# A longer lag for the mixer steps that run beside the products of a hybrid block

## The chip, the cores and the metric

The kernel runs on one core of one Trainium2 chip. The metric is the device time of one execution in microseconds. Of the kernel before, three runs are known, with a median of 3934.16 us.

## What is computed

Two blocks of two layers each work on one sequence of 1024 tokens with 1024 features. Block 1, which the change is about, runs three mixers side by side in each layer and joins them in one output product:

```python
def hybrid_layer(x, c_act, ...):
    h = rms_norm(x, pre_gain) * (1.0 + scale) + shift
    aq, ak, av, ag, rq, rk, rv, rg, gq, gk, gv, gg, ga = split(h @ w_in)
    a_out = sliding_window_attention(rotary(aq), rotary(ak), av, sinks) * silu(ag)
    r_out = rms_norm(retention(rotary(rq), rotary(rk), rv)) * silu(rg)
    g_out = rms_norm(gated_linear_attention(gq, gk, gv, log_a), gain) * silu(gg)
    y = concatenate([a_out, r_out, g_out]) @ w_out
    return x + gate * rms_norm(y, post_gain)
```

Attention looks back over a window of 128 tokens; retention and gated linear attention (GLA) carry a state from chunk to chunk. Block 2 (attention with a context, spatial gating, a Fourier mixer, and a squared ReLU network) follows on the result.

## The kernel before

Tokens are worked on in tiles of 128, four tiles to a group, so block 1 has four steps: two layers by two groups. All large products are made in float32 from two float32r parts, which gives three matmuls for each pair of operands. `product` (L467) walks over the eight 128-row slices of the inner dimension. For each slice it loads a weight tile into `wr`, makes its high part `wh` on ScalarE and its low part `wl` on VectorE (L202, L203), and issues the matmuls (L502), 12 for four outputs. After each slice it calls `tick`.

The mixers have no products of their own to wait in. They are generators in a list `bg`, and `tick` lets the first of them run up to its next `yield`. So a mixer's program is spread over the slices of the products that are made meanwhile: `s_attn` beside `p_ret`, `s_ret` beside `p_gla`, and `s_gla` beside the next step's `p_attn`, or, in the last step, beside two early products of block 2. A piece that feeds matmuls from VectorE or ScalarE runs one `yield` ahead of the piece that uses it: in `s_attn` `scores(i)` before `values(i - 1)`, in `s_ret` `values(i - 1)` before `into(i - 2)`, in `s_gla` `level(i)` before `scores(i - 1)`. `into` (L534) transposes a finished head and splits it into `mT`, the left operand of the output product. `aside` advances the modulation vectors (L311, L316, L317, L283), which are also worked on in the background.

The order of the instructions on each engine is not the program's order alone. A scheduler issues an instruction when it thinks its operands ready, and takes the earlier one in the program first where several are. Some pieces have a higher priority (`high_priority`): the weight splits most of all.

A tile's tag names its pool and the number of its buffers. The tags that matter here: `sc` for scores and other products of a mixer step, `st` for the GLA score matrices and masked queries, `pe` for temporaries of the evacuations (rotary, norm, gating), and in PSUM `mm` (4 banks) for the products, `sm` (2 banks) for scores, their transposes and state updates, `o` (1 bank) for the values. Stores of tiles to the device's memory are issued by POOL (L579), whose descriptors lie in a scratch that takes 16 KB of each partition unless a size is given.

A GLA unit `level` makes two differences on POOL (L983, L984), their exponential on ScalarE (L985), `kl` (L987) and `ql` (L989) on VectorE. `scores` multiplies them (L997) and copies the result under a mask into the score matrix (L1000). There are seven levels for each of two halves.

Of the kernel before, what the change touches and what calls it, by code (L numbers as in the profile page):

```python
# [25 lines left out]
GT = 4  # L26
# [136 lines left out]
class Net:  # L163
    HP, HE, HX = 3000, 800, 600

    def __init__(self, ctx, tc, a):
        self.tc, self.nc, self.a = tc, tc.nc, a
        self.ctx = ctx
        self.n = 0
        self.bg = []  # L170
        self.pools = {}
        mk = lambda name, tags, **kw: self.open(ctx, name, tags, **kw)
        self.cpool = ctx.enter_context(tc.tile_pool(name="cst", bufs=1))
        self.dpool = ctx.enter_context(tc.tile_pool(name="dr", bufs=1, space=DRAM))
        mk("small", {"ti": 14, "tm": 16, "md": 4, "ab": 6, "pad": 1})
        self.T("pad", [P, 8])
        mk("big", {"wr": 3, "wl": 4, "wh": 4, "x": 4, "pe": 3,
                   "H": 16, "M": 4, "pt": 8, "kv": 2})
        mk("ps", {"mm": 4, "mt": 1, "sm": 2, "o": 1}, space=PSUM)

# [526 lines left out]
    def s_attn(self, l, g, st, mT):  # L707
        nc = self.nc
# [63 lines left out]

        units = [(t, e) for t in range(GT) for e in range(2)]
        ready = []
        for i in range(len(units) + 1):
            if i < len(units):
                scores(*units[i])
                yield True
            if i:
                values(*units[i - 1])  # L780
                t, e = units[i - 1]
                if e:
                    ready.append((t, close(t)))
                elif ready:
                    self.into(mT, 0, ready[0][0], ready.pop(0)[1], 4)
                yield True
                if i % 4 == 3:
                    self.aside()
        yield True
        self.into(mT, 0, ready[0][0], ready[0][1], 4)  # L790

    def p_ret(self, l, g, hT, st):
        nc, w = self.nc, self.a["w_in"][l]
# [36 lines left out]
    def s_ret(self, l, g, st, mT):  # L830
        nc = self.nc
# [42 lines left out]
            return self.head_norm(O, sg[t])  # L874

        sc, y = [None] * GT, [None] * GT
        for i in range(GT + 2):
            if i > 1:
                self.into(mT, 4, i - 2, y[i - 2], 2)
            if 0 < i <= GT:  # L880
                y[i - 1] = values(i - 1, *sc[i - 1])
            if i < GT:
                sc[i] = scores(i)
            yield True
            if i in (2, 4):
                self.aside()
                yield True
# [47 lines left out]
    def s_gla(self, l, g, st, mT):  # L935
# [86 lines left out]
            return self.head_norm(O, sg[t])  # L1022

        units = [(u, n, s) for u in range(2) for n, s in enumerate((64, 32, 16, 8, 4, 2, 1))]
        y, made = [None] * GT, None
        for i in range(len(units) + 1):
            if i:
                scores(*units[i - 1], *made)
            if i < len(units):
                made = level(*units[i])  # L1030
            if i in (9, 11):
                y[i // 2 - 4] = values(i // 2 - 4)
            if i in (11, 13):
                self.into(mT, 6, i // 2 - 5, y[i // 2 - 5], 2)
            yield True
            if i % 7 in (2, 5):
                self.aside()
        for i in range(2, GT + 2):
            if i < GT:
                y[i] = values(i)  # L1040
            if i > 3:
                self.into(mT, 6, i - 2, y[i - 2], 2)
            yield True
            if i in (2, 4):
                self.aside()
# [5 lines left out]
    def block1(self, cur, n_layers, after=True):  # L1051
        a = self.a
        self.first = True
        with ExitStack() as ctx:
            self.open(ctx, "b1", {"gt": 2, "ys": 4, "ac": 1, "aw": 4, "pu": 12, "st": 3, "sc": 5, "rs": 2, "gs": 2, "gb": 2, "gq": 2, "dg": 2}, {"row": "x"})
            self.cpool = ctx.enter_context(self.tc.tile_pool(name="c1", bufs=1))
            self.cst1 = self.C(CST1.shape)
            self.load(self.cst1[:, :64], a["cst1"][:, :64])
# [671 lines left out]
```

## Time and profile before

| | us |
|---|---|
| median of three runs | 3934.16 |
| lowest and highest run | 3931.94, 3938.04 |
| the profiled execution | 3937.08 |
| its span, from the first to the last instruction | 3935.3 |
| TensorE busy | 3726.1 (95%) |
| VectorE busy | 2445.6 (62%) |
| ScalarE busy | 1685.8 (43%) |
| GpSimd (POOL) busy | 649.3 (17%) |

Busy times are sums over the whole span and say little about one stage. Block 1 takes about the first 1215 us of it. A wait is put down to the engine and instruction that ended it; matmuls follow each other in a pipeline, so a matmul's duration is longer than its distance to the next.

### The profile page before, as it was taken

To read this page: it belongs to the slowest core of one execution; us is meant where nothing else is said; L and a number is where in the kernel's file an instruction comes from. 1 tells how busy PE (TensorE), PEld (TensorE's weight loads), DVE (VectorE), ACT (ScalarE), POOL (GpSimd) and SP (SyncE) were. 2 spreads that over 40 slices of the span, in tenths; PEclk is the share of its full clock that TensorE was granted. 3 is DMA by queue.
4 is the path that set the end of the run, shared out by engine and by line. 5 is a ranking of instruction groups with operands and counts; after the bars stand their busy time and mean duration, and the time that the engine had idled before them with its cause. 6 is when DMAs were issued, how large, how long until landed. Compare 5 with 4: busy or idle time off the path is not lost. (4 is left out here: it accounts for less than half of the span.)

```text
span 3935.3 us, 55613 instructions
## 1 busy us (share of the span) xinstructions
PE 3726.1 (95%) x19144; PEld 3045.4 (77%) x19144; DVE 2445.6 (62%) x5209; ACT 1685.8 (43%) x3652; POOL 649.3 (17%) x1026
## 2 busy tenths in 40 slices
PE   7999999999999898899999999999899999999998
PEld 6877777877877787677887788888777788887886
DVE  7686787687687657576545643335765654455444
ACT  4443444454454555464334422224554543344333
POOL 2021134243252212131001000000311100001000
PEclk9999999999999999999999999999999999999999
DMA  6144344343343313333333632222412123334332
GB/s 213 50 134 121 113 143 121 109 129 110 105 136 98 103 56 107 108 108 105 126 102 110 209 110 68 62 66 89 145 54 86 69 64 97 97 100 166 97 97 94
DMA packets 249453, 420.37 MB, mean 107 GB/s; under 512 B 32002, under 2 KB 101203, under 8 KB 249171
## 3 DMA queue, kind: packets, MB, share of 16 engines
q1 hardware_dynamic: 241426, 389.52, 32.0%
q0 software_dynamic: 7744, 27.30, 1.9%
q8 instruction: 151, 2.47, 0.3%
q14 instruction: 132, 1.07, 0.1%
HBM read 389.42 MB, written 27.30 MB: 106 GB/s over the span
## 5 line engine op out<-in xcount | busy, mean ns | idle before, releaser
L203 DVE TENSOR_TENSOR wl<-wr,wh 128x512 fp32r<-128x512 f32 (+2 forms) x948 | 644.2, 682 | 812.9 <-ACT wh L202 809.4
L202 ACT CAST wh<-wr 128x512 fp32r<-128x512 f32 (+2 forms) x948 | 553.7, 585 | 1208.8 <-PE mm L502 489.8
L502 PE MATMUL mm<-wh,M 128*128 128x512 f32 (+1 forms) x2944 | 945.9, 393 | 24.6 <-ACT M L202 14.8
L502 PE MATMUL mm<-wh,H 128*128 128x512 f32 (+2 forms) x2432 | 791.5, 396 | 12.3 <-DVE pe L654 3.6
L506 PE MATMUL mm<-H,wh 128*128 128x512 f32 x2240 | 727.4, 395 | 1.8 <-ACT wh L202 1.7
L502 PEld LDWEIGHTS mm<-wh,M 128*128 128x128 f32 x2944 | 550.0, 190 | 142.8 <-ACT M L202 23.1
L502 PE MATMUL mm<-wl,M 128*128 128x512 f32 (+1 forms) x1472 | 576.0, 391 | 0.4 <-DVE wl L203 0.4
L502 PEld LDWEIGHTS mm<-wh,H 128*128 128x128 f32 x2432 | 450.0, 192 | 100.5 <-issue 4.7
L506 PEld LDWEIGHTS mm<-H,wh 128*128 128x128 f32 x2240 | 418.8, 189 | 82.2 <-ACT wh L202 2.0
L502 PE MATMUL mm<-wl,H 128*128 128x512 f32 (+2 forms) x1216 | 471.1, 388 | 0.0
L506 PE MATMUL mm<-H,wl 128*128 128x512 f32 x1120 | 444.5, 397 | 0.0
L502 PEld LDWEIGHTS mm<-wl,M 128*128 128x128 f32 x1472 | 279.8, 190 | 49.2 <-DVE wl L203 1.2
L502 PEld LDWEIGHTS mm<-wl,H 128*128 128x128 f32 x1216 | 234.0, 192 | 35.1 <-issue 0.2
L506 PEld LDWEIGHTS mm<-H,wl 128*128 128x128 f32 x1120 | 212.2, 189 | 37.2
L1398 PEld LDWEIGHTS o<-kv,pT 128*128 128x128 f32 x1280 | 158.1, 192 | 25.0 <-ACT pT L1394 20.4
L317 POOL TENSOR_TENSOR ac<-ac,aw 128x256 f32<-128x256 f32 x168 | 142.9, 851 | 162.8 <-ACT aw L316 143.9
L1398 PE MATMUL o<-kv,pT 128*128 128x64 f32 x1280 | 167.5, 274 | 1.6 <-ACT pT L1394 0.9
L311 DVE SCALAR_TENSOR_TENSOR ac<-aw,c,ac 128x256 f32<-128x256 f32 x280 | 160.1, 572 | 5.9 <-DMA aw<-in_w_ada 3.1
L1483 DVE TENSOR_TENSOR Z<-Z,mm 128x512 f32<-128x512 f32 x224 | 140.2, 681 | 2.8 <-PE mm L502 2.5
L558 POOL TENSOR_TENSOR tm<-tm 128x1 f32<-128x1 f32 x34 | 6.6, 196 | 763.3 <-ACT pe L553 762.9
L1375 DVE CUSTOM_DVE_ANT_0 p<-sm,c,c 128x384 f32<-128x384 f32 (+1 forms) x144 | 82.2, 571 | 76.0 <-PE sm L1373 74.5
L1381 ACT ACTIVATE p<-p,ti 128x640 f32<-128x640 f32 (+2 forms) x144 | 110.8, 770 | 43.1 <-DVE ti L1380 39.7
(353 smaller groups left out, 5703.1 us busy)
## 6 DMA issues: line engine op xcount, KB each, us to landing
wr<-in_w_ff SPq DMA_DIRECT2D x512, 256.0 KB, 2.7
wr<-in_w_in SPq DMA_DIRECT2D x240, 256.0 KB, 2.7
wr<-in_w_out SPq DMA_DIRECT2D x144, 256.0 KB, 2.7
x<-xd SPq DMA_DIRECT2D x64, 512.0 KB, 4.9
aw<-in_w_ada SPq DMA_DIRECT2D x192, 128.0 KB, 2.1
x<-in_w_ada SPq DMA_DIRECT2D x96, 256.0 KB, 2.9
xd<-x POOLq DMA_DIRECT2D x44, 512.0 KB, 3.8
wr<-in_w_in SPq DMA_DIRECT2D x152, 128.0 KB, 2.1
```

Of the source, the lines that this page charges most:

```text
L202: self.nc.scalar.copy(hi, src)
L203: self.nc.vector.tensor_sub(lo, src, hi.bitcast(F32))
L311: nc.vector.scalar_tensor_tensor(acc[:, 0], wt, c[0], acc[:, 0], ALU.mult, ALU.add)
L317: nc.gpsimd.tensor_tensor(acc[:, 1], acc[:, 1], wt, ALU.add)
L502: nc.tensor.matmul(acc[j][:, :ncol], lhsT=x[:, j * P:(j + 1) * P], rhs=y[:, :ncol], start=first, stop=last)
L506: nc.tensor.matmul(acc[j][:m, :w], lhsT=y[:, j * P:j * P + m], rhs=x[:, :w], start=first, stop=last)
L558: nc.gpsimd.tensor_tensor(ss[j][:, 0:1], ss[j][:, 0:1], ss[j][:, 1:2], ALU.add)
L1375: nc.vector.tensor_tensor_reduce(sc[:, at:at + w], ps[:, :w], mask, 1.0, prev, ALU.add, ALU.max, accum_out=acc)
L1381: nc.scalar.activation(sc[:, :at], sc[:, :at], AF.Exp, bias=nm, accum_out=den[:, h:h + 1])
L1398: nc.tensor.matmul(O[:, h * 64:h * 64 + 64], lhsT=pT[:, i, :], rhs=Vs(j)[:, sl], start=i == 0, stop=i == nk - 1)
L1483: nc.vector.tensor_add(y, y, ps)
```

## The change

Three mixers wait longer. In `s_attn` `values` runs two units behind `scores`, and `into` follows when the next tile closes. In `s_ret` `into` runs two steps behind `values`. In `s_gla` `scores` runs two levels behind `level`, kept in a list `made`, and `into` one step later. The calls of `aside` in `s_attn` leave the inner condition. The scratch for the descriptors shrinks from 16 KB to 4 KB per partition; the 12 KB go to one more `pe` buffer (2 KB), one more `st` (4 KB) and three more `sc` (2 KB each).

```diff
-        mk("big", {"wr": 3, "wl": 4, "wh": 4, "x": 4, "pe": 3,
+        mk("big", {"wr": 3, "wl": 4, "wh": 4, "x": 4, "pe": 4,
                    "H": 16, "M": 4, "pt": 8, "kv": 2})
...
-        for i in range(len(units) + 1):
+        for i in range(len(units) + 2):
             if i < len(units):
                 scores(*units[i])
                 yield True
-            if i:
-                values(*units[i - 1])
-                t, e = units[i - 1]
+            if i > 1:
+                values(*units[i - 2])
+                t, e = units[i - 2]
                 if e:
+                    if ready:
+                        self.into(mT, 0, *ready.pop(), 4)
                     ready.append((t, close(t)))
-                elif ready:
-                    self.into(mT, 0, ready[0][0], ready.pop(0)[1], 4)
                 yield True
-                if i % 4 == 3:
-                    self.aside()
+            if i % 4 == 3:
+                self.aside()
         yield True
-        self.into(mT, 0, ready[0][0], ready[0][1], 4)
+        self.into(mT, 0, *ready.pop(), 4)
...
-        for i in range(GT + 2):
-            if i > 1:
-                self.into(mT, 4, i - 2, y[i - 2], 2)
+        for i in range(GT + 3):
+            if i > 2:
+                self.into(mT, 4, i - 3, y[i - 3], 2)
...
-        y, made = [None] * GT, None
-        for i in range(len(units) + 1):
-            if i:
-                scores(*units[i - 1], *made)
+        y, made = [None] * GT, []
+        for i in range(len(units) + 2):
+            if i > 1:
+                scores(*units[i - 2], *made.pop(0))
             if i < len(units):
-                made = level(*units[i])
+                made.append(level(*units[i]))
             if i in (9, 11):
-                y[i // 2 - 4] = values(i // 2 - 4)
-            if i in (11, 13):
-                self.into(mT, 6, i // 2 - 5, y[i // 2 - 5], 2)
+                y[(i - 9) // 2] = values((i - 9) // 2)
+            if i in (12, 14):
+                self.into(mT, 6, (i - 12) // 2, y[(i - 12) // 2], 2)
...
-        for i in range(2, GT + 2):
+        for i in range(2, GT + 3):
             if i < GT:
                 y[i] = values(i)
-            if i > 3:
-                self.into(mT, 6, i - 2, y[i - 2], 2)
+            if i > 4:
+                self.into(mT, 6, i - 3, y[i - 3], 2)
...
-            self.open(ctx, "b1", {"gt": 2, "ys": 4, "ac": 1, "aw": 4, "pu": 12, "st": 3, "sc": 5, "rs": 2, "gs": 2, "gb": 2, "gq": 2, "dg": 2}, {"row": "x"})
+            self.open(ctx, "b1", {"gt": 2, "ys": 4, "ac": 1, "aw": 4, "pu": 12, "st": 4, "sc": 8, "rs": 2, "gs": 2, "gb": 2, "gq": 2, "dg": 2}, {"row": "x"})
...
-    nc = _bacc.Bacc("TRN2", target_bir_lowering=False, num_devices=1)
+    nc = _bacc.Bacc("TRN2", target_bir_lowering=False, num_devices=1, dynamic_dma_scratch_size=4096)
```

Every engine has the same instructions as before, in another order. Line numbers in the excerpts of the order are those of the kernel before; the changed functions keep them to within two lines, and the lines named here are the same in both.

First excerpt: VectorE in the second step, at the second GLA level. `sc_5684` is its `ql`, and the copy of its scores is the one that reads `sm_5705`. The L311 rows are modulation. Before:

```order
L989 TENSOR_TENSOR sc_5684<-st_5642,sc_5678 128x512
L311 SCALAR_TENSOR_TENSOR ac_5187<-aw_5191,c_70,ac_5187 128x256
L1000 COPY_PREDICATED st_5640<-c_629,sm_5674 128x8x64
L311 SCALAR_TENSOR_TENSOR ac_5187<-aw_5194,c_70,ac_5187 128x256
L1000 COPY_PREDICATED st_5640<-c_629,sm_5705 128x16x32
L311 SCALAR_TENSOR_TENSOR ac_5187<-aw_5197,c_70,ac_5187 128x256
L987 TENSOR_TENSOR sc_5713<-pt_4840,sc_5709 128x256
L311 SCALAR_TENSOR_TENSOR ac_5187<-aw_5200,c_70,ac_5187 128x256
L989 TENSOR_TENSOR sc_5715<-st_5642,sc_5709 128x512
```

With the change the same level's `ql` is `sc_5680`, and its scores are read from `sm_5779`:

```order
L989 TENSOR_TENSOR sc_5680<-st_5642,sc_5674 128x512
L1000 COPY_PREDICATED st_5640<-c_629,sm_5701 128x8x64
L311 SCALAR_TENSOR_TENSOR ac_5182<-aw_5189,c_70,ac_5182 128x256
L987 TENSOR_TENSOR sc_5709<-pt_4840,sc_5705 128x256
L311 SCALAR_TENSOR_TENSOR ac_5182<-aw_5192,c_70,ac_5182 128x256
L989 TENSOR_TENSOR sc_5711<-st_5642,sc_5705 128x512
L311 SCALAR_TENSOR_TENSOR ac_5182<-aw_5195,c_70,ac_5182 128x256
L1000 COPY_PREDICATED st_5640<-c_629,sm_5779 128x16x32
```

The next level's `ql` now stands ahead of the copy, where it stood behind it.

Second excerpt: TensorE in the third step's retention, from `values` of the second tile (L860, L862, into `o_4949`) to the transposes of the first tile's head `sc_4911` (L524). Before:

```order
L860 MATMUL o_4949<-rs_1934,sc_4930 128x128 x2
L862 MATMUL o_4949<-pu_4821,st_4921 128x64 x4
L502 MATMUL mm_5393<-wh_5396,H_2256 128x512
L502 MATMUL mm_5393<-wl_5397,H_2256 128x512
L502 MATMUL mm_5393<-wh_5396,H_2257 128x512
L524 MATMUL sm_4944<-c_76,sc_4911 128x128 x2
L867 MATMUL sm_4956<-pu_4821,pu_4411 128x128 x2
```

With the change, where the second tile's values go into `o_4944` (L506 is a product too, the last half of an output product):

```order
L862 MATMUL o_4944<-pu_4821,st_4921 128x64 x4
L846 MATMUL sm_4969<-pt_4414 128x128 x2
L506 MATMUL mm_4841<-H_2265,wh_5106 128x512
L506 MATMUL mm_4841<-H_2265,wl_5107 128x512
L506 MATMUL mm_4841<-H_2266,wh_5106 128x512
L506 MATMUL mm_4842<-H_2265,wh_5106 128x512
L506 MATMUL mm_4842<-H_2265,wl_5107 128x512
L846 MATMUL sm_4973<-pt_4414 128x128 x2
L506 MATMUL mm_4842<-H_2266,wh_5106 128x512
L502 MATMUL mm_5387<-wh_5391,H_2251 128x512
L283 MATMUL o_4991<-c_76,ac_4721 128x1 x2
L524 MATMUL sm_5032<-c_76,sc_4911 128x128 x2
```

The transposes stand behind the third tile's scores (L846), where they stood ahead of them.

## Rows read from the trace of the kernel before

**Rows 1.** The page: the span, and its part 1, the engines' busy time.
```profile
span 3935.3 us, 55613 instructions
...
PE 3726.1 (95%) x19144; PEld 3045.4 (77%) x19144; DVE 2445.6 (62%) x5209; ACT 1685.8 (43%) x3652; POOL 649.3 (17%) x1026
```

**Rows 2.** TensorE's waits, 100 to 1215 us: releaser; us in total, times, longest us.
```profile
PE sm L997 <- DVE sc L989: 19.6, 22, 2.4
PE sm L524 <- DVE sc L827: 10.8, 8, 1.9
PE o L1014 <- DVE st L1000: 6.0, 6, 2.2
PE mm L502 <- DVE pe L654: 3.6, 4, 2.5
PE sm L746 <- ACT sc L736: 3.0, 4, 1.1
...
PE mm L502 <- ACT wh L202: 0.8, 1, 0.8
```

**Rows 3.** Busy time by stretch: block 1, then four GLA stretches and their sum.
```profile
core 0: us, PE busy (x) PEld busy (x) DVE busy (x) ACT busy (x) POOL busy (x), PEclk, DMA share, GB/s
100.00:1215.00 1115.00, 1054.67 (x5677) 854.35 (x5675) 859.07 (x1886) 517.60 (x1268) 341.96 (x484) 0.99 0.38 115
...
260.00:340.00 80.00, 75.38 (x394) 61.74 (x395) 73.90 (x192) 29.75 (x67) 19.47 (x34) 1.00 0.50 154
540.00:650.00 110.00, 95.09 (x482) 75.87 (x481) 99.88 (x224) 54.82 (x124) 52.42 (x75) 0.98 0.45 133
840.00:945.00 105.00, 93.69 (x480) 74.79 (x481) 93.23 (x211) 54.52 (x120) 49.79 (x68) 0.98 0.37 106
1140.00:1220.00 80.00, 68.93 (x356) 54.30 (x355) 67.29 (x130) 37.76 (x90) 46.78 (x67) 0.98 0.36 109
sum 375.00, PE 333.09 PEld 266.70 DVE 334.31 ACT 176.85 POOL 168.46; mean PE 83.27 PEld 66.67 DVE 83.58 ACT 44.21 POOL 42.12
```

**Rows 4.** VectorE's groups, 540 to 640 us: busy us, mean ns | idle before, releaser.
```profile
L311 DVE SCALAR_TENSOR_TENSOR ac<-aw,c,ac 128x256 f32<-128x256 f32 x44 | 27.2, 617 | 0.2
...
L1000 DVE COPY_PREDICATED st<-c,sm 128x512 f32<-128x512 uint8 x14 | 12.3, 882 | 1.2 <-PE sm L997 1.2
L989 DVE TENSOR_TENSOR sc<-st,sc 128x512 f32<-128x512 f32 x14 | 11.3, 806 | 0.0
L987 DVE TENSOR_TENSOR sc<-pt,sc 128x256 f32<-128x256 f32 x13 | 7.2, 557 | 1.4 <-ACT sc L985 1.4
```

**Rows 5.** Product matmuls (L502) alone, in 20 us of undisturbed products: TensorE busy and count.
```profile
960.00:980.00 20.00, 20.00 (x90) 16.38 (x89) 1.00 0.44 132
```

**Rows 6.** VectorE's waits, 100 to 1215 us, those that ScalarE and POOL end.
```profile
DVE sc L827 <- POOL ti L209: 15.7, 15, 1.7
...
DVE sc L987 <- ACT sc L985: 10.0, 15, 1.8
```

**Rows 7.** TensorE's waits in the whole span: the product behind block 2's gated unit.
```profile
PE mm L502 <- DVE pe L1241: 7.7, 4, 2.6
```

**Rows 8.** TensorE's timeline at block 1's end: start us, us; L502 is the output product.
```profile
1211.39 0.62 PE L502 MATMUL mm<-wh,M 128*128 128x512 f32 x2
...
1213.32 1.00 PE L1014 MATMUL o<-pu,st 128*128 128x64 f32 x8
```

**Rows 9.** POOL's tile stores (L579): duration ns min/median/max, and who waited for them.
```profile
L579 POOL DMA_DIRECT2D xd<-x x44: 531/628/1086, 396.0 to 3542.3; - x44
...
  DVE x L377: 9.4, 3
```

**Rows 10.** VectorE's timeline, 820 to 850 us: splits of 128x272; start us, us.
```profile
828.50 0.43 DVE L203 TENSOR_TENSOR wl<-wr,wh 128x272 fp32r<-128x272 f32 x1
...
842.16 4.49 DVE L203 TENSOR_TENSOR wl<-wr,wh 128x272 fp32r<-128x272 f32 x3 [0.76 <-ACT wh L202]
```

**Rows 11.** POOL's timeline in the same stretch: start us, us.
```profile
844.26 2.09 POOL L973 TENSOR_TENSOR st<-c,dg 128x1024 f32<-128x1024 f32 x1
```

## The prediction

> **What bounds the kernel now.** I read the page's busy shares first. TensorE is busy for 95% of the span and VectorE for 62% [rows 1], so only TensorE's idle time can be won: 209 us in all (3935.3 - 3726.1). The change sits in block 1, so I then asked who ended TensorE's waits between 100 and 1215 us. The list is short [rows 2]: the GLA score matmuls (L997) wait 19.6 us for the masked queries of L989, the transposes that carry a finished head into mT (L524) wait 10.8 us for the last step of the head norm (L827), the GLA values 6.0 us, the attention transposes (L746) 3.0 us. Weights are no issue: the product waited 0.8 us once for a split.
>
> Third I asked where this happens. Of the 60 us that TensorE idles there (1115 - 1054.7), nearly all but 18 lie in four stretches in which the GLA mixer runs beside the products that follow it [rows 3]. They take 375 us, with TensorE busy for 333.1 and VectorE for 334.3: TensorE idles 41.9 us, VectorE 40.7 us. So two engines bound these stretches together, and hand work back and forth one step apart.
>
> **Lag of the GLA scores.** A unit is: two subtractions on POOL, exp on ScalarE, `kl` (L987, 0.56 us) and `ql` (L989, 0.81 us) on VectorE, two L997 matmuls, and the predicated copy L1000 (0.88 us) [rows 4]. No instruction is added or removed; `scores` merely comes two levels behind `level`. A product step is 12 matmuls, and 90 of them start in 20 us [rows 5], so a step is 12 x 20 / 90 = 2.7 us, longer than the longest L997 wait of 2.4 us [rows 2]. If program order set the instruction order, all 19.6 us would go. It doesn't: the scheduler issues a row when it thinks its input is there, and VectorE's order shows what is left of the lag (the first excerpt of the order). Between a `ql` and the copy that reads its scores there stood 3 rows in that place and now 6; over all 56 units I count 8.3 and 15.9 rows on average. The span in which TensorE may run the scores without holding up VectorE has thus about doubled, but TensorE's row still follows closely on its `ql`. Ends: 0 and 19.6 us. VectorE's own idle time in block 1 ends mostly on ScalarE and POOL (10.0 us for L987, 15.7 us for L827) [rows 6], which the lag doesn't touch, so I take less than half: **-8**.
>
> **Lag of `into`** (retention and GLA heads one more step behind `values`). The longest of the 8 waits on L827 is 1.9 us, less than a step of 2.7 us [rows 2, 5]. In the second excerpt of the order three product rows stood between `values` and the transposes of the head before, now seven, with two more score groups. Other heads move less, since the scheduler had let product rows in before. Ends 0 and 10.8: **-5**.
>
> **Lag of the attention values**: ends 0 and 3.0 [rows 2], and the probabilities of a unit are exponentials that are now a unit older: **-1.5**.
>
> **What comes nearer.** `values(0)` of GLA ran two steps behind the last scores of its half; these now come a step later and `values(0)` doesn't, so one step of cover goes. The nearest row is L1014's wait on L1000, longest 2.2 us [rows 2]. Four steps of the block have such a head: between 0 and 4 x 2.2 = 8.8. One step of 2.7 us is left, which is more than a wait of 2.2: **+2**.
>
> **The fourth `pe` buffer**, the only size that also acts in block 2. Rows that could owe their wait to a missing buffer: products on the rotary's reads (3.6) [rows 2], and products on the gated unit's evacuation in block 2 (7.7) [rows 7]. Ends 0 and 11.3. Nearly all of it is VectorE's own chain, which a buffer doesn't shorten: **-1**.
>
> **Ticks.** A step's mixers need 17 + 9 + 22 = 48 product ticks where they needed 17 + 8 + 20 = 45. GLA has 24 ticks in the first three steps and fits. In the last it has 16, so six ticks instead of four are left for the drain. What covers them are the first matmuls of the output product, which stand between the last scores and values [rows 8]; without that cover it would be two steps, 5.4 us: **+1.5**. The background modulation chunks are started as often as before, in attention one tick earlier; their loads pass others on SP's queue, and a late weight would show as the 0.8 us row of [rows 2]: 0.
>
> **The descriptor scratch.** 44 tile stores between layers go through POOL's software queue, 0.53 to 1.09 us each, median 0.63, and only three times did someone wait for one [rows 9]. If a smaller ring made each as slow as the slowest, POOL would work 20 us more (44 x 0.46), off the path but for those three, 1.4: between 0 and 1.4, I take 0, since nothing in the trace comes near a queue of many stores.
>
> **Sum**: -8 - 5 - 1.5 + 2 - 1 + 1.5 = -12.0 us. The profiled execution took 3937.1 us (span 3935.3 and 1.8 around it), 2.9 above the median of the runs, so 3925.1 against 3937.1 and **3922** against the median of 3934.2. What a measurement can tell from no change here is about 0.2%, 7.9 us.
>
> **Rival 1: the wait only moves.** VectorE is busy for 89% of the four stretches, and its rows are long there. The plainest case [rows 10, 11]: three splits of 128x272 took 4.49 us, 1.50 each, while POOL ran products over 128x1024 of 2.09 us; the same split took 0.43 us some 14 us earlier. If VectorE's pace under POOL's work sets the stretch, an order with more room between its rows changes which TensorE row waits and not how long: the lag terms go to zero, leaving +2 - 1 + 1.5, so 3937, and with a few us won, 3930. For it: the near equal idle times [rows 3]. Against it: that idle time exists at all; a bound engine would have none. The Trainium skill (SBUF — State Buffer, "SBUF: two separate sides") says that VectorE and GpSimd share a port pair under an exclusive lock, so that one waits for the other's whole instruction; the long splits beside POOL's long rows agree with it, and by it this rival's 3937 would be the forecast. Chance 0.30, for 3926 to 3942.
>
> **Rival 2: the score banks become the wait (slower).** The scores, their transposes and the state updates share two PSUM banks (`sm`). With more VectorE rows between a `ql` and the copy that empties the bank, a score row may find both banks full and wait for the copy of the unit before. Price per unit: the `kl`, `ql` and one modulation row that now stand ahead of that copy, 0.56 + 0.81 + 0.62 = 2.0 us [rows 4]. Six of the 56 units eat the forecast's gain; twelve give 24 - 12 = 12 us slower, 3946. For it: in the first excerpt of the order the next `ql` stands ahead of the copy. Against it: VectorE waited only 1.2 us in 100 for score matmuls [rows 4], so the copy runs as soon as VectorE gets to it. Chance 0.20, with what else a rescheduled program may lose.
>
> **Rival 3: more than forecast.** If all rows on which L997, L524 and L746 wait were early enough, 19.6 + 10.8 + 3.0 = 33.4 us would go instead of 14.5, which gives 3903. It would need VectorE about 98% busy in the stretches (334.3 of 375 - 33.4). It is in the 0.50 for faster, as its far end, at about 0.08.
>
> **How the numbers follow.** Forecast and rival 3: 0.50, faster by over 0.2%. Rival 1, read as within 0.2%: 0.30. Rival 2: 0.20. The likeliest case alone spans 3908 to 3926. The range reaches from rival 3's 3903, a little further down, to rival 2's 3946; I leave out some 0.08 below and 0.10 above. A change of order alone can move a 3934 us program by some us either way; that is in the width.
>
> **What would show it.** Right: in the list of waits L997 on L989 near 12 us instead of 19.6 and L524 on L827 near 6; the four stretches shorter by 12 us in all, VectorE's busy share there above 90%; counts of instructions equal. Wrong by rival 1: stretches as long as before, the waits on other tiles. Wrong by rival 2: L997 waiting for `st` L1000, and in sum more than 20 us. Wrong altogether: a gain or loss in block 2, where only the `pe` buffer and the scheduler's order act, or store issues on POOL well over 0.63 us.

## The result, and the profile after

The changed kernel takes 3957.5 us (median of four runs, 3946.5 to 3959.5) against 3933.4 for the kernel before, a ratio of 1.0053 with a 95% interval of 1.0033 to 1.0074. The forecast was 3922 and the range ended at 3946: wrong in direction and outside the range.

The page's first lines already tell where the loss is not. The span and part 1 of the profile after:

```profile
span 3957.3 us, 55517 instructions
...
PE 3745.2 (95%) x19144; PEld 3064.9 (77%) x19144; DVE 2436.9 (62%) x5209; ACT 1687.2 (43%) x3652; POOL 653.6 (17%) x1026
```

TensorE runs the same 19144 matmuls, yet is busy for 19.1 us longer (3745.2 against 3726.1 [rows 1]). Its idle time, which the whole forecast was about, went from 209.2 us (3935.3 - 3726.1) to 212.1 (3957.3 - 3745.2). So of the 22.0 us between the two spans, 2.9 are idle time and 19.1 are the same work done more slowly. Inside block 1 idle time grew too: from 60.3 us in 100 to 1215 us [rows 3] to 70.9 (1145 - 1074.1) in the same work after the change.

```profile
100.00:1245.00 1145.00, 1074.13 (x5686) 873.96 (x5684) 854.67 (x1886) 519.74 (x1270) 347.22 (x485) 0.97 0.37 111
```

TensorE's waits in the profile after, 100 to 1245 us, which is the work that took until 1215 us before (releaser; us in total, times, longest us):

```profile
PE sm L997 <- DVE sc L989: 8.4, 7, 1.8
PE o L283 <- DVE ac L311: 5.7, 6, 1.6
PE sm L997 <- DVE M L203: 4.9, 3, 3.2
PE sm L524 <- DVE sc L827: 4.5, 5, 1.5
PE mm L502 <- DVE pe L654: 4.0, 2, 2.1
PE mm L502 <- DVE pu L544: 3.8, 2, 2.2
PE sm L524 <- DVE st L847: 3.6, 2, 2.1
PE o L1014 <- DVE st L1000: 3.5, 6, 1.0
PE sm L524 <- DVE gs L1021: 3.0, 2, 1.6
PE sm L524 <- POOL sc L770: 3.0, 3, 1.2
PE o L283 <- POOL ac L317: 2.6, 4, 1.2
PE mt L398 <- DVE x L377: 2.5, 7, 0.6
...
PE sm L997 <- DVE st L1000: 2.1, 3, 1.2
```

Compare with [rows 2]. Every wait that the change aimed at shrank, by more than forecast: L997 on L989 from 19.6 to 8.4 us, L524 on L827 from 10.8 to 4.5, and L746 on L736 (3.0) is gone. L1014 on L1000, which was to grow, fell from 6.0 to 3.5; 23.0 us in all. Others grew in their place, most of them on rows of VectorE: modulation (L311 was 1.7), a split of mT (`M` L203), an evacuation (L544 was 0.8), a mask (L847), a state update (L1021); two are on POOL (L770, L317). Added up by the row that waits, whatever it waits for, the score matmuls (L997) went only from 22.2 us to 17.3, the transposes into `sm` (L524) from 11.9 up to 14.1, and the modulation's own matmuls (L283) from 3.1 to 9.6.

To see it by stage I cut both traces where the same product matmuls stand, counted from the start: a stretch ends with the last matmul of the same product in both. First the three stretches in which the GLA mixer runs beside the next step's attention projections, before the change, then after it (busy us of each engine; the granted clock, as a share of TensorE's full 2.4 GHz; DMA share; GB/s):

```profile
252.50:348.60 96.10, 89.58 (x486) 73.78 (x485) 86.17 (x218) 39.00 (x89) 24.93 (x38) 1.00 0.48 149
534.90:641.50 106.60, 91.80 (x478) 73.73 (x476) 97.86 (x218) 53.24 (x121) 48.73 (x66) 0.98 0.48 141
837.30:942.20 104.90, 93.57 (x489) 75.08 (x489) 93.13 (x213) 54.82 (x123) 49.24 (x67) 0.98 0.37 109
sum 307.60, PE 274.96 PEld 222.59 DVE 277.16 ACT 147.06 POOL 122.90; mean PE 91.65 PEld 74.20 DVE 92.39 ACT 49.02 POOL 40.97
```

```profile
254.60:352.20 97.60, 89.97 (x484) 74.05 (x482) 84.77 (x212) 38.93 (x88) 25.12 (x38) 0.99 0.47 145
541.40:649.30 107.90, 94.41 (x478) 76.22 (x476) 95.52 (x219) 53.24 (x120) 47.64 (x65) 0.95 0.46 134
850.80:958.50 107.70, 95.84 (x502) 78.28 (x502) 94.24 (x216) 55.35 (x125) 51.36 (x69) 0.97 0.38 111
sum 313.20, PE 280.23 PEld 228.55 DVE 274.53 ACT 147.51 POOL 124.13; mean PE 93.41 PEld 76.18 DVE 91.51 ACT 49.17 POOL 41.38
```

TensorE idles 32.6 us there before (307.6 - 275.0) and 33.0 after (313.2 - 280.2), though the waits on L989 halved. What grew is its busy time, by 5.3 us, and in the last column before the DMA share one sees most of the reason: the granted clock fell to 0.95 in the second stretch and 0.97 in the third. The third also holds 13 matmuls more than before.

The four stretches beside the retention mixer (GLA's own projections), their sum before, then after:

```profile
sum 240.70, PE 231.72 PEld 184.03 DVE 206.59 ACT 121.26 POOL 79.82; mean PE 57.93 PEld 46.01 DVE 51.65 ACT 30.31 POOL 19.96
```

```profile
sum 254.10, PE 235.21 PEld 187.39 DVE 211.23 ACT 124.71 POOL 86.28; mean PE 58.80 PEld 46.85 DVE 52.81 ACT 31.18 POOL 21.57
```

These lost 13.4 us, and here it is mostly idle time that grew, from 9.0 to 18.9 us; the busy time grew by 3.5 us, with 49 more matmuls in these stretches. The last stretch beside GLA (block 2's first early product), before and after:

```profile
1136.10:1202.70 66.60, 58.18 (x311) 47.37 (x312) 58.63 (x106) 36.23 (x87) 42.53 (x58) 0.97 0.41 123
```

```profile
1158.80:1232.10 73.30, 64.54 (x315) 53.91 (x316) 58.87 (x113) 36.58 (x87) 42.68 (x58) 0.88 0.34 101
```

6.7 us longer, of which 6.4 are busy time at a granted clock of 0.88 instead of 0.97. The output products behind the first three GLA stretches lost 5.4 us (141.9 to 147.3), at a clock of 0.94 to 0.96 where it was 1.00, and retention's projections gained 0.8. That makes the 30 us by which block 1 ends later than before: some 19 of them busy time, 11 idle time. Block 2 takes 8 us less than in the profile before, nearly all of it in one stretch at its start, which took 489.8 us before and 482.2 after. The change can hardly be the reason: with the smaller scratch alone, every engine in its old order, that stretch took 486.6 us, and in no other profile of this document more than 486.5.

What TensorE did before its clock fell can be seen at the beginning of that stretch, in the timeline of the profile after (start us, us; the idle time before an instruction and its releaser in brackets):

```profile
1156.82 0.39 PE L502 MATMUL mm<-wh,H 128*128 128x512 f32 x1
1158.81 0.39 PE L502 MATMUL mm<-wh,H 128*128 128x256 f32 x1 [1.59 <-DVE pu L544]
```

The same place by windows:

```profile
1136.00:1160.00 24.00, 20.30 (x105) 15.93 (x104) 20.45 (x42) 13.95 (x35) 10.64 (x15) 1.00 0.54 170
1160.00:1166.80 6.80, 6.80 (x34) 6.80 (x33) 1.25 (x5) 2.77 (x7) 3.25 (x4) 0.50 0.13 40
```

In the 24 us before, TensorE was idle for 3.7, and one wait of 1.59 us for the evacuation L544 stood at the end; then the clock was granted at half (1.2 GHz) for 6.8 us. That wait belongs to the list of new ones above.

### The profile page after: what moved, and what is told of

Read it like the earlier page. It is cut to its first block, busy times and chain, and to the rows that moved or that the text cites. A ratio compares the mean times of both kernels' runs of the same rounds, so it can differ in the third digit from the quotient of the medians.

```text
span 3957.3 us, 55517 instructions
## 1 busy us (share of the span) xinstructions
PE 3745.2 (95%) x19144; PEld 3064.9 (77%) x19144; DVE 2436.9 (62%) x5209; ACT 1687.2 (43%) x3652; POOL 653.6 (17%) x1026
## 5 line engine op out<-in xcount | busy, mean ns | idle before, releaser
L203 DVE TENSOR_TENSOR wl<-wr,wh 128x512 fp32r<-128x512 f32 (+2 forms) x948 | 636.6, 673 | 819.8 <-ACT wh L202 812.9
L502 PE MATMUL mm<-wh,M 128*128 128x512 f32 (+1 forms) x2944 | 950.4, 395 | 22.5 <-ACT M L202 14.0
L502 PE MATMUL mm<-wh,H 128*128 128x512 f32 (+2 forms) x2432 | 791.6, 397 | 14.6 <-DVE pe L654 4.0
L506 PE MATMUL mm<-H,wh 128*128 128x512 f32 x2240 | 729.7, 396 | 1.9 <-ACT wh L202 1.8
L502 PEld LDWEIGHTS mm<-wh,M 128*128 128x128 f32 x2944 | 552.0, 191 | 140.3 <-ACT M L202 22.2
L502 PE MATMUL mm<-wl,M 128*128 128x512 f32 (+1 forms) x1472 | 577.2, 392 | 0.8 <-DVE wl L203 0.8
L502 PEld LDWEIGHTS mm<-wh,H 128*128 128x128 f32 x2432 | 454.7, 194 | 103.7 <-issue 6.7
L506 PEld LDWEIGHTS mm<-H,wh 128*128 128x128 f32 x2240 | 419.4, 189 | 82.1 <-ACT wh L202 2.3
L502 PE MATMUL mm<-wl,H 128*128 128x512 f32 (+2 forms) x1216 | 477.1, 393 | 2.3 <-DVE wl L440 2.3
L506 PE MATMUL mm<-H,wl 128*128 128x512 f32 x1120 | 444.6, 397 | 0.0
L502 PEld LDWEIGHTS mm<-wl,M 128*128 128x128 f32 x1472 | 281.2, 191 | 50.6 <-DVE wl L203 1.0
L502 PEld LDWEIGHTS mm<-wl,H 128*128 128x128 f32 x1216 | 236.3, 194 | 39.9 <-DVE wl L440 3.2
L506 PEld LDWEIGHTS mm<-H,wl 128*128 128x128 f32 x1120 | 212.2, 189 | 37.7
L317 POOL TENSOR_TENSOR ac<-ac,aw 128x256 f32<-128x256 f32 x168 | 144.0, 857 | 159.7 <-ACT aw L316 131.4
L311 DVE SCALAR_TENSOR_TENSOR ac<-aw,c,ac 128x256 f32<-128x256 f32 x280 | 159.8, 571 | 7.2 <-DMA aw<-in_w_ada 3.5
L1394 ACT COPY pT<-sm 128x512 f32<-128x512 f32 (+1 forms) x144 | 80.2, 559 | 115.8 <-PE sm L524 115.5
```

Of the source, the lines that this page charges most:

```text
L203: self.nc.vector.tensor_sub(lo, src, hi.bitcast(F32))
L311: nc.vector.scalar_tensor_tensor(acc[:, 0], wt, c[0], acc[:, 0], ALU.mult, ALU.add)
L317: nc.gpsimd.tensor_tensor(acc[:, 1], acc[:, 1], wt, ALU.add)
L502: nc.tensor.matmul(acc[j][:, :ncol], lhsT=x[:, j * P:(j + 1) * P], rhs=y[:, :ncol], start=first, stop=last)
L506: nc.tensor.matmul(acc[j][:m, :w], lhsT=y[:, j * P:j * P + m], rhs=x[:, :w], start=first, stop=last)
L1394: nc.scalar.copy(pT[:, c0:c0 + n, :], tp)
```

## Experiments, first group: which part costs

All kernels of this section and the next have the smaller descriptor scratch. Each is compared with runs of the kernel before on the same chip.

**Scratch alone** (order of every engine unchanged).

```diff
-num_devices=1)
+num_devices=1, dynamic_dma_scratch_size=4096)
```

> The kernel before with the smaller descriptor scratch alone; every engine keeps its order. If the scratch costs (POOL slower at issuing stores, or transfers that start late): 3940 to 3957 us, with POOL's stores (L579) above a median of 0.63 us. If the loss lies in the order of instructions, as I hold: 3933, within 4 us, the stores as long as before.

Measured: 0.9997 (0.9987 to 1.0008). POOL's stores have the same durations as in [rows 9], to 2 ns:

```profile
L579 POOL DMA_DIRECT2D xd<-x x44: 533/628/1086, 395.3 to 3542.3; - x44
```

The scratch costs nothing.

**All added buffers, no lag.**

```diff
-"pe": 3   "st": 3, "sc": 5
+"pe": 4   "st": 4, "sc": 8
```

> The kernel before with the smaller scratch and all the added buffers (pe 4, st 4, sc 8), all lags as before. Theory A (the longer lags cost, by new waits in block 1 and the clock that falls around them): within 4 us of 3933, granted clock near .986. Rival B (the buffers cost: the scheduler uses the room to run VectorE's rows ahead of those that TensorE needs): 3950 to 3957, clock near .980. Rival C (any re-ordering of block 1 loses, since the order before happens to be a good one): somewhere between, 3938 to 3950.

Measured: 1.0033 (1.0021 to 1.0046), 3946.2 us, in rival C's range and near B's. Theory A falls: more than half of the loss comes without any lag.

**The fourth `pe` alone, and eight `sc` alone.**

> The kernel before with the smaller scratch and the fourth pe buffer alone. The three added sizes together cost 0.33% (13 us), most of it in block 1. Theory D (the fourth pe buffer is what costs: it lets the scheduler put evacuations of a later product ahead of mixer rows on VectorE, in all stages): 3943 to 3948. Rival E (the room for scores, sc 8, or for the state, st 4, costs): within 5 us of 3934 here.

> The kernel before with the smaller scratch and eight sc buffers alone. Rival E (room for more scores lets VectorE's and ScalarE's mixer rows run ahead of those that TensorE needs): 3941 to 3948. Theory D (it is the pe buffer): within 4 us of 3934; few rows move, since the order differs little from the one before.

Measured: 1.0004 (0.9995 to 1.0013) for `pe`, 1.0018 (1.0009 to 1.0027) for `sc`. Theory D falls, and E's price holds; room for scores costs, though in the traces only some 200 of VectorE's 5209 rows change places. For `pe` nothing in all need not mean nothing anywhere: in its one profile block 1 and its last output product take 1275.6 us against 1262.6 before and 1265.7 with the scratch alone, and the rest is shorter than in either. `st` alone was not run.

**GLA's lag, and attention's with retention's, each on top of the buffers.** The diff of the change in `s_gla` alone, and in `s_attn` and `s_ret` alone:

```diff
-                scores(*units[i - 1], *made)        (GLA's)
+                scores(*units[i - 2], *made.pop(0))
...
-                values(*units[i - 1])               (attention's)
+                values(*units[i - 2])
-                self.into(mT, 4, i - 2, y[i - 2], 2)    (retention's)
+                self.into(mT, 4, i - 3, y[i - 3], 2)
```

> Scratch and buffers as with the change, and of the lags only GLA's (scores two levels behind, into one step later); attention and retention as before. Theory A1 (GLA's lag costs): 3950 to 3957, the stages with attention's projections longer by 1 to 3 us each, as with the change, the wait of L997 on L989 near 8 us. Theory A2 (the lags of attention and retention cost, GLA's helps as predicted): 3922 to 3930, L997 on L989 near 8 us as well. Rival C (any re-ordering loses): 3938 to 3957.

> Scratch and buffers as with the change, and the lags of attention and retention without GLA's. Theory A1 (GLA's lag costs): within 5 us of 3933. Theory A2 (these two cost): 3950 to 3957, the stages with the projections of GLA and retention longer, as with the change (59 to 62, 58 to 60, 62 to 66, 61 to 66 us beside the retention mixer), and L997 on L989 still near 20 us. Rival C: 3938 to 3957 here too, whatever the part.

Measured: 1.0030 (1.0018 to 1.0042) with GLA's, 1.0042 (1.0030 to 1.0055) with the other two. On top of 1.0033 for the buffers GLA's lag is worth nothing and the other two cost perhaps 0.1%, which is within the intervals. GLA's time (3946.3 us) is in neither range of theories A1 and A2, only in rival C's; that of the other two (3951.2) is in A2's range and in C's, and the four stretches beside retention are long as A2 had it (253.6 us in all).

**The lags without the buffers**: all three, then each alone, by the same edits.

```diff
-"pe": 4   "st": 4, "sc": 8
+"pe": 3   "st": 3, "sc": 5
```

> All three lags as with the change, the smaller scratch, but all buffers as before (pe 3, st 3, sc 5). If buffers and lags cost independently, the lags alone are worth 0.53% - 0.33% = 0.20%: 3942, from 3937 to 3947. If the lags only lose because of the fourth pe buffer: 3934 or less. If the lags need the buffers (with five sc and three st the longer queue of scores holds back POOL and VectorE): above 3957.

> The kernel before with the smaller scratch and GLA's lags alone, buffers as before. On top of the added buffers this part cost nothing (3946.3 against 3946.2 us). If it is worth nothing by itself too: 3934, within 4 us, with the wait of L997 on L989 at 8 us and as much again in new waits. If my price of it (8 us) held and the buffers ate it: 3922 to 3929. If it needs the sc and st buffers: 3938 to 3948.

> The kernel before with the smaller scratch and attention's lag alone, modulation where it was. GLA's alone cost 0.13%, retention's alone 0.15%, all three 0.21%. If the parts add up: 0.07% below before, 3931 to 3935. If any re-ordering costs its 0.1 to 0.2%: 3938 to 3943.

> The kernel before with the smaller scratch and retention's lag alone (into two steps behind values). All lags together cost 0.21%, GLA's alone 0.13%. If retention's costs (the four stages with GLA's projections became 1.6 to 5.2 us longer with the change): 3937 to 3944, those stages longer in the same way. If it is attention's: within 3 us of 3934.

Measured: all three 1.0021 (1.0011 to 1.0031); GLA's alone 1.0013 (1.0003 to 1.0024); attention's alone 1.0000 (0.9991 to 1.0010); retention's alone 1.0015 (1.0006 to 1.0024). All three came out where adding up puts them (3942 expected, 3944.7 measured), attention's alone near its figure. Retention's alone cost what was expected (3943.4 us), but not where: the four stretches beside it take 241.9 us against 240.7 before, while the third GLA stretch takes 113.0 against 104.9, at a clock of 0.94. Attention's alone does lengthen the stretches beside retention, to 245.6 us, and wins that back elsewhere:

```profile
sum 245.60, PE 234.10 PEld 187.41 DVE 206.12 ACT 123.66 POOL 83.35; mean PE 58.53 PEld 46.85 DVE 51.53 ACT 30.91 POOL 20.84
```

For GLA's lag alone the time (3940.9) falls into the range for "needs the buffers", but it gains nothing with them either, so that reading falls. So lags 0.21% and buffers 0.33% add up to the 0.53% of the change, within the noise; the lags don't need the buffers, and no part gains. The run with GLA's lag alone shows the wait of L997 on L989 at 14.6 us instead of 19.6, and the same three GLA stretches:

```profile
sum 315.60, PE 279.27 PEld 227.74 DVE 275.94 ACT 146.20 POOL 122.40; mean PE 93.09 PEld 75.91 DVE 91.98 ACT 48.73 POOL 40.80
```

TensorE idles 36.3 us in them (315.6 - 279.3), against 32.6 without the lag. A lag that removes its own wait wins nothing in total.

## Experiments, second group: is VectorE the bound?

If VectorE's load sets the GLA stretches, the lag should gain once that load is smaller. L311, the modulation, is 28 us of VectorE's time in 107 and need not stand there: 47 rows in the second stretch of the kernel before.

```profile
L311 DVE SCALAR_TENSOR_TENSOR ac<-aw,c,ac 128x256 f32<-128x256 f32 x47 | 28.6, 609 | 0.2
L203 DVE TENSOR_TENSOR wl<-wr,wh 128x512 fp32r<-128x512 f32 x19 | 15.1, 804 | 1.6 <-ACT wh L202 1.4
```

**Modulation moved away from the GLA mixer, alone, with all lags, and with the whole change.**

```diff
-                if i % 4 == 3:                  (s_attn)
+                if i in (3, 4, 5, 7):
...
-            if i % 7 in (2, 5):                 (s_gla)
-                self.aside()
...
-            if i in (2, 4):                     (s_gla)
-                self.aside()
...
+    def s_side(self, n):
+        for _ in range(n):
+            self.aside()
+            for _ in range(4):
+                yield True
...
                 if pend:
+                    self.bg.append(self.s_side(4))
                     finish(*pend)
+                    self.drain()
```

> The kernel before with the smaller scratch and its modulation chunks moved: none beside the GLA mixer, twice as many in attention, four beside each output product. This takes some 27 us of L311 out of every 100 us of the GLA stretches. Theory V (VectorE's load there sets the stretches, so a longer lag had nothing to win): TensorE's 41.9 us of idle time in the four stretches fall below 25, and the kernel takes 3910 to 3925. Rival R (the round trip from one mixer row to the next sets them, VectorE's load does not): within 5 us of 3934, the wait of L997 on L989 still near 20 us. Rival C (any re-ordering loses): above 3938.

> The same move of the modulation with all three lags, buffers as before. Under the old modulation the lags cost 0.21%. Theory V: with VectorE free in the stretches the lags work as they were meant to: 5 to 12 us below the run with the moved modulation alone. If the lags lose for another reason (retention's and attention's stages, where VectorE was not full): 5 to 10 us above it.

> The whole change with the same move of the modulation. The change without the move cost 0.53%. Theory V: most of that goes, within 8 us of the run with the moved modulation alone, on either side. If buffers and lags cost by themselves, whatever VectorE has to do: 15 to 23 us above it.

Measured: 1.0023 (1.0010 to 1.0036), 1.0017 (1.0005 to 1.0028) and 1.0040 (1.0026 to 1.0054). The first (3947.5 us) is far from theory V's 3910 to 3925; the second lies 2.7 us below it instead of 5 to 12, and only the third, 6.0 us above it, is within V's 8. The trial had a fault: four chunks fewer were called, and they stood at block 1's end. There the output product took 86 us instead of 60; its stretch before, and with the modulation moved:

```profile
1202.70:1262.40 59.70, 53.91 (x265) 40.98 (x264) 42.39 (x118) 25.96 (x67) 9.27 (x19) 0.97 0.31 99
```

```profile
1191.90:1278.10 86.20, 62.94 (x283) 49.41 (x282) 52.09 (x139) 36.42 (x86) 25.15 (x37) 0.78 0.31 99
```

Up to that point the kernel was 11 us ahead (1191.9 against 1202.7), so the trial was repeated with nothing left over.

**Modulation moved, none left over.**

```diff
-                if i in (3, 4, 5, 7):
+                if i in (3, 5, 7):
...
+            if g and l and i % 7 in (2, 5):     (s_gla, last step only)
+                self.aside()
...
-                    self.bg.append(self.s_side(4))
+                    self.bg.append(self.s_side(5))
```

> As the run with the moved modulation, but none of it left over for the end: three chunks in attention, two in retention, five beside each output product, and beside the GLA mixer only in the last step, as before the change. That run was 11 us ahead of the kernel before when block 2's first product was done and lost 27 us in the output product behind it, where the left-over chunks stood. Theory V (VectorE's load in the GLA stretches sets them): 3915 to 3926, the three stretches of the first steps 5 to 12 us shorter each, the end of block 1 as before. Rival (modulation costs wherever it stands, a gain comes back as a loss): 3932 to 3942.

> Moved modulation with GLA's lags, and buffers as before (pe 3, st 3, sc 5). Lag and the st and sc buffers together gained 0.31% over before, the moved modulation alone nothing. If the lag is what gains once VectorE has room: 3924 to 3930 here. If it needs the buffers to hold the queries and scores that wait longer: 3932 to 3940.

> Moved modulation with the st and sc buffers of the change and no lag. If the lag is what gains: 3934 to 3945, no better than without the buffers (in the old order the sc buffers alone cost 0.18%). If the buffers are what gains: 3924 to 3930.

> The same, with GLA's lags and the st and sc buffers of the change, but not the lags of attention and retention nor the fourth pe buffer. With the modulation out of the way the lag's stretches were 1 to 4 us shorter each with the buffers than without lag. If the lag needs a VectorE with room (theory V): 5 to 10 us below the run with the moved modulation alone. If it only adds waits, as it did in the old order: 3 to 10 us above it.

> The same as the run before with attention's lag too; only retention's lag and the fourth pe buffer are left out of the change. If attention's lag helps where VectorE carries more modulation (with four chunks the retention projections took 80 to 90 us with it, 86 to 93 without): 3 to 8 us below the run without it. If its wait of 3 us was all there was to win: within 4 us of it.

The edits of the last four are this one with GLA's lag, with `"st": 4, "sc": 8`, with both, and with attention's lag besides; the fourth `pe` and retention's lag are in none.

| with the modulation moved | ratio to before |
|---|---|
| no lag, old buffers | 0.9999 (0.9990 to 1.0009) |
| GLA's lag, old buffers | 0.9954 (0.9942 to 0.9967), 3919.7 us |
| no lag, `st` 4 and `sc` 8 | 0.9983 (0.9974 to 0.9992) |
| GLA's lag, `st` 4 and `sc` 8 | 0.9969 (0.9955 to 0.9983) |
| the same with attention's lag | 0.9992 (0.9978 to 1.0006) |

The move alone came out as its rival said (3937.2 us), the lag on top better than expected (3919.7), the buffers alone between the two readings (3931.9), both together 13 us below the move alone, where theory V had 5 to 10, and attention's lag against its expectation: 8 us slower, not 3 to 8 faster, though the two intervals touch.

The three GLA stretches with the modulation moved, without and with GLA's lag:

```profile
253.10:346.30 93.20, 86.38 (x464) 71.94 (x463) 70.99 (x173) 39.22 (x87) 21.52 (x37) 1.00 0.34 100
...
sum 288.40, PE 265.18 PEld 219.28 DVE 224.69 ACT 123.31 POOL 76.55; mean PE 88.39 PEld 73.09 DVE 74.90 ACT 41.10 POOL 25.52
```

```profile
sum 279.50, PE 262.50 PEld 217.76 DVE 220.90 ACT 122.64 POOL 79.62; mean PE 87.50 PEld 72.59 DVE 73.63 ACT 40.88 POOL 26.54
```

VectorE's share fell from 90% (277.2 of 307.6) to 78% (224.7 of 288.4). The stretches became 19.2 us shorter by the move, and another 8.9 with the lag, TensorE's idle time there going from 32.6 to 23.2 and 17.0 us. VectorE was not relieved alone: the rest of the modulation moved with L311, so POOL's work in these stretches fell from 122.9 to 76.6 us, ScalarE's from 147.1 to 123.3, and the DMA share by a quarter or more. The wait of L997 on L989 shows the same step, 100 to 1205 us, without and with the lag:

```profile
PE sm L997 <- DVE sc L989: 20.2, 21, 2.5
```

```profile
PE sm L997 <- DVE sc L989: 10.3, 11, 2.0
PE o L755 <- DVE sc L748: 5.8, 8, 1.7
```

So the lag cuts its own wait in the old order and halves it in this one; only here does the time follow. How much of the time is the lag's is less sure than the table says. The profile of the move alone is its fastest execution, 3927.4 us at a granted clock of 0.987, where its twelve runs reach 3943.3 and 0.980. Between the two profiles the lag is worth 6.7 us, between the medians 17.5, and the five runs with the lag had 0.985 to 0.988. So a part of the medians' difference came with the clock. Nor is the lag alone in shortening these stretches: `st` 4 and `sc` 8 without it do as much (TensorE idle for 16.9 us), yet gain only 0.16% in all.

```profile
sum 279.70, PE 262.79 PEld 219.78 DVE 223.81 ACT 122.40 POOL 77.24; mean PE 87.60 PEld 73.26 DVE 74.61 ACT 40.80 POOL 25.75
```

The move alone still gains nothing: modulation now stands beside attention, and the three stretches of retention's projections take that back. Their sums before, with the move, and with the move and the lag:

```profile
sum 252.70, PE 248.58 PEld 203.75 DVE 173.56 ACT 106.53 POOL 52.85; mean PE 82.86 PEld 67.92 DVE 57.85 ACT 35.51 POOL 17.62
```

```profile
sum 268.00, PE 255.29 PEld 209.97 DVE 192.19 ACT 117.97 POOL 79.04; mean PE 85.10 PEld 69.99 DVE 64.06 ACT 39.32 POOL 26.35
```

```profile
sum 269.50, PE 258.52 PEld 211.58 DVE 193.01 ACT 118.39 POOL 78.11; mean PE 86.17 PEld 70.53 DVE 64.34 ACT 39.46 POOL 26.04
```

15 and 17 us longer. With the lag the page of the best kernel reads:

```profile
span 3918.9 us, 55654 instructions
...
PE 3722.6 (95%) x19144; PEld 3051.6 (78%) x19144; DVE 2435.1 (62%) x5209; ACT 1684.5 (43%) x3652; POOL 646.9 (17%) x1026
```

TensorE's idle time is 196.3 us, 12.9 below the kernel before. That is near the forecast's 12.0 by chance: one lag of the three is in it, and the modulation had to go out of the way first. This kernel, GLA's lag with the moved modulation and the old buffers, beats both: the kernel before by 0.46%, and the changed one by about 1% (0.9954 / 1.0053 = 0.990).

The buffers gain 0.16% without the lag here and lose 0.15% with it, the latter within the intervals, and attention's lag on top loses 0.23%, at their edge. In the old order the buffers lost 0.33%, `pe` included: the worth of such a part depends on the order that it meets.

## Why the prediction was wrong, step by step

- **The sum.** Idle time was to fall by 12.0 us and rose by 2.9, and 19.1 us of busy time came on top, for which the sum had no term. Two steps failed: that a wait that is removed is time that is gone, and that the busy time stays ("only TensorE's idle time can be won").
- **Lag of the GLA scores, -8.** As a wait it was right and more (-11.2). As time it was 0 or worse: alone it made 1.0013. (The counts of 8.3 and 15.9 rows take in one end; the excerpt's 3 and 6 do not.) The step that failed is "I take less than half" of a wait in a stretch where VectorE is 90% busy. The runs show that the value hangs on what else stands in the stretch: nothing with VectorE at 90%, 0.45% with it at 78% (0.9999 without the lag, 0.9954 with it), or 17.7 us, a part of them the clock's. That it is VectorE's load and not POOL's or the DMA's, which fell with it, is argued and not shown.
- **Rival 1, the wait only moves**, was the case as far as idle time in the GLA stretches goes: 32.6 us before, 33.0 after, on other tiles. That is its mark but for the length, which grew by 5.6 us. Its argument against itself, "a bound engine would have none" of the idle time, was the mistake that held its chance at 0.30: before and after, both engines were idle for about a tenth of these stretches (VectorE for 30.4 and 38.7 us), and yet shorter waits won nothing. Its price of 3937 lacked what the clock took: with the 11 to 19 us estimated below it is 3948 to 3956.
- **Lag of `into`, -5, and of the attention values, -1.5.** The waits fell by 6.3 and 3.0. But the transposes that `into` makes (L524) wait longer in sum, as said above: the wait was renamed. Alone, retention's lag costs 0.15% and attention's nothing. Both together lengthen the stretches beside retention: 240.7 us before, 241.9 with retention's lag alone, 245.6 with attention's alone, 252.5 with all three lags and the old buffers, 253.6 with these two and the new ones, 254.1 after the change. Attention's program has 17 ticks in both kernels, but its pieces come later in them: with its lag 120 of its value matmuls (L755, L757) fall into these stretches where 64 did, and 16 more transposes. New waits come with them, on POOL's L770 (2.4 us with attention's lag alone, 3.0 after the change, none before) and on L377 (2.6 and 2.5). Retention's program, now 9 ticks, ends a tick later, and the wait on its mask L847 (none before) grows from 1.7 to 3.6 us. "Ticks: +1.5", which looked at the last step alone, was the mis-sized term: these stretches lost 13.4 us.
- **`values(0)` nearer, +2.** L1014 on L1000 fell from 6.0 to 3.5. No cost.
- **The fourth `pe`, -1.** 1.0004 (0.9995 to 1.0013): nothing in all. The other two sizes had no term at all, since they were read as room for the lag; in the old order `sc` alone costs 0.18%, and the three sizes without a lag 0.33%, more than half of the loss. Room changes what the scheduler does even where no lag uses it.
- **The scratch, 0.** Right.
- **Rival 2, the score banks**, gave the time nearest to the result (3946), by a mechanism that did not happen: L997 waited for `st` L1000 for 2.1 us in all, not for more than 20.
- **A gain or loss in block 2.** The loss is in block 1 alone; the 8 us that block 2's profile is shorter by stand for the most part where the scratch alone, with the order unchanged, is shorter too.

The second missing term is the clock. By the clock that the traces record, TensorE was busy at half the clock for 90.1 us before and for 135.2 after. If work takes twice as long there, half of that is what the low clock cost, and without it 3681.1 and 3677.6 us of busy time are left: the clock accounts for all of the growth. Each profile's span times its mean granted clock is also nearly the same for kernels whose times differ. Span and mean clock before, after, and with the three lags alone:

```profile
core 0: 3935.3 us, clock 0.986
```

```profile
core 0: 3957.3 us, clock 0.980
```

```profile
core 0: 3946.5 us, clock 0.982
```

The products are 3880, 3878 and 3876 us, each within 2 by the rounding of the clock. One kernel's own executions come near to this with their order fixed: the twelve of the lags alone have spans from 3934.1 us to 3949.5, at 0.986 to 0.982, and products from 3875 to 3883. It is a rough rule: the twelve of the move alone have products from 3858 to 3875. The best kernel has 3918.9 at 0.985, a product of 3860, so most of its gain is not the clock's.

How large the clock's part of the loss is depends on the execution. In the profiled one the busy time grew by 19.1 us. But the fastest of the four, at 0.985 nearly the clock of the kernel before, still took 3946.5 us, 13 more than that kernel and 11 less than the median. So the clock's part is estimated at 11 to 19 us of the 24. What makes it fall more often under the change is only argued: in the case above a wait from the new list stood just ahead. No run held the waits fixed and changed the clock.

## What to carry to other kernels

Before a wait between two engines is priced, read the busy share of both in that stretch: here, at 90% on the engine that is waited for, a longer lag renamed the wait. Take work out of that stretch first, then try the lag again. Price moved waits in sum over the stretch (length less busy time), never by their names in the list. A reordering can also move the granted clock: read the clock column by stretch, and compare runs at the same clock before a difference of some tenths of a per cent is put down to a cause.

## What the runs showed of the hardware

- TensorE's busy time for the same 19144 matmuls differs by 29 us between kernels that only order them differently: 3719.9 us with the modulation moved alone (mean granted clock 0.987), 3745.2 after the change (0.980), 3748.6 with the whole change and the first move of the modulation (0.975). In the example above the clock fell behind waits of which none was longer than 1.6 us. The Trainium skill (TensorE: Matmul & The Clock Gate, "What's actually happening") says that the gate follows how busy the engine has been of late; a fall right behind a wait fits that.
- VectorE's split of a weight tile (L203, 128x512) took 804 ns on average in the second GLA stretch before and 720 with the modulation moved, while POOL's work in it fell from 48.7 us to 30.9:

```profile
L203 DVE TENSOR_TENSOR wl<-wr,wh 128x512 fp32r<-128x512 f32 x20 | 14.3, 720 | 6.2 <-ACT wh L202 6.0
```

The Trainium skill (SBUF — State Buffer, "SBUF: two separate sides") has VectorE and GpSimd share a port pair; fewer POOL rows beside shorter splits agree with it, but the modulation rows moved with them, so the runs don't separate the two.
